# Moving preparation steps between the down-projection stages of a fused ConvFFN kernel

## The chip, the cores and the metric

The kernel runs on one core of one Trainium2 chip. Its time is the device time of one execution in microseconds (us), given as the median of several runs. A profiled execution, taken by the hardware profiler, supplies the trace: its span runs from the first to the last instruction.

## The reference, cut to what matters

One decoder layer over 512 prompt tokens and 8 x 8 sample tokens (576 columns in all, width 1024). What the change touches is the last part, a convolutional feed-forward network (2816 hidden columns, 22 tiles of 128), and, by way of the scheduler, the attention.

```python
def _layer(x, c, ...):
    h = _rmsnorm(x, norm1_g) * (1.0 + sc1) + sh1
    b_gate, c_gate, xa, q, k, v, ga, gb = jnp.split(h @ w_in, cuts, axis=-1)
    ...                                          # short convolution, attention, two gates
    x = x + g1 * (mixed @ w_mix_out)
    h2 = _rmsnorm(x, norm2_g) * (1.0 + sc2) + sh2
    a, val = jnp.split(h2 @ w_up, 2, axis=-1)
    ac, new_ffn = _causal_conv(a, ffn_buf, ffn_conv_w)       # 3 taps per channel
    x = x + g2 * ((jax.nn.gelu(ac, approximate=False) * val) @ w_down)
    return x, ...
```

All is float32.

## The kernel before, in words

**Layout.** Activations lie transposed: 128 channels on the partitions, the 576 tokens along the free axis. A float32 product is made of three TensorE passes in `fp32r`: each operand is split into a high part (`hi`, a copy rounded to fp32r) and a low part (`lo`, what the rounding left), and hi x hi, hi x lo and lo x hi are added up in PSUM.

**Seven products for eight.** The feed-forward works on pairs: two weight tiles by the two halves of the tokens (288 columns each), and two halves of the summed axis. `pair_product` does such a block with seven products where the plain way takes eight, from sums and differences of weights (A, B, C, D) and of activations. It runs seven *parts*, numbered 0 to 6, in three PSUM banks: X, Z, Y, X, Y, Z, Y. Y is a row `mm` in the profile, X and Z are `aux`; a copy of Z in SBUF is `p` (`p5`). Between the parts, small operations carry one bank into another:

| after part | operation | row in the profile | what needs it |
|---|---|---|---|
| 0 | ACT, `minus(Y, X)`: Y becomes -X | `mm<-aux` | part 2, which adds into Y |
| 1 | ACT, copy of Z to `p5` | `p<-aux` | `minus(Z, Y)`, which writes Z; the outputs after parts 4 and 5 |
| 2 | ACT, `minus(Z, Y)`: Z becomes -Y | `aux<-mm` | part 4, which adds into Y; part 5, which adds into Z |
| 3 | DVE, `out_a0(X)` | `x<-aux` in down stages | |
| 4 | DVE, `out_b1(Y, p5)` reads Y | `p<-mm` in down stages | part 6, which adds into Y |
| 5, 6 | DVE, `out_a1(Z, p5)`, `out_b0(Y)` | | |

In up stages a part is 12 matmuls, in down stages 9.

**Steps.** A stage's `steps[k]` are emitted ahead of part k (`steps[7]` after the last). Here stands the work for the *next* stage: its weights are read, summed and split while this stage multiplies. `pair_weights(ra, rb, moved)` gives the pieces: `ah`/`al` the high and low part of A (from `ra`), `sums1` two DVE sums (D's, and B's, in place in `rb`), `bh`/`bl` B, `sums2` two more DVE sums for C, `dh`/`dl` D (half as wide; rows `wh`, `wl`, `s`), `ch`/`cl` C. A high part is one ACT copy (`whi<-raw`). A low part is a DVE subtraction (`wlo<-raw,whi`). For a name in `moved` it is made without DVE: ACT writes minus the high part (`wlo<-whi`), then a DMA that POOL issues adds the raw weights to it (the profile's DMA row `wlo<-raw`, or `wl<-s` for D); I call it that name's *transfer*.

**The stages.** `order` runs the up tiles 4 to 10 (each with a gate and a value half), then four down stages m = 0, 2, 4, 6 over the first six hidden tiles (`FA = 6`), then the up tiles 11 to 21. An up stage's work beside the product comes from `beside_pair`: A at step 0, B's high part at 1, its low part at 2, D from 3, C at 5, and between them the convolution of the tile before: `first_tap` (ACT, `y<-pad,par2T`), `taps` (two DVE operations, `y<-pad,par2T,y`), `gelu`, `times`, `high`. A down stage's work comes from `beside_down(t, summed)`: the first down stage makes `sums1` itself (`summed` false); the other three find it made, at step 6 of the stage before. Tile 10's convolution is left over when the down stages begin; `first_ops` puts its taps into the second down stage and its GELU and multiplication into the third.

**What sets the order.** From the feed-forward on, PE, ACT and DVE are *pinned*: they run their instructions in the order in which the code emits them, by the helper at line 115 (so nearly every profile row has line 115). An instruction that waits thus holds all behind it on its engine. The parts before, the attention among them, are ordered by a scheduler's estimates, which know the pools of buffers. Tiles of 576 columns come from one pool of `A_BUFS` buffers (*slots*), taken in turn; a taker waits until the last user of its slot is done. Four raw weight tiles (`raw`) and five each of `whi` and `wlo` are in flight.

Of the kernel before, what the change touches and what calls it, by code (L numbers as in the profile page):

```python
# [10 lines left out]
F32 = mybir.dt.float32  # L11
# [5 lines left out]
P = 128  # L17
D = 1024
# [11 lines left out]
DOWN_AT = 11  # L30
# [6 lines left out]
CACHE_AT = 17,18  # L37
EPS = 1e-6
NEG = -1e33
A_BUFS = 57  # L40
W_BUFS = 4
S_BUFS = 5
HT = NT // 2
# [32 lines left out]
def step_kernel(ctx: ExitStack, tc: tile.TileContext, ins: dict, outs: list):  # L76
# [4 lines left out]
    cp = ctx.enter_context(tc.tile_pool(name="cp", bufs=1))  # L81
    ap_ = ctx.enter_context(tc.tile_pool(name="ap", bufs=A_BUFS))
    wp = ctx.enter_context(tc.tile_pool(name="wp", bufs=3))
# [12 lines left out]
    def slot(s, dt=F32, shape=None):  # L96
        return ap_.tile(shape or [P, NT], dt, tag="a", name=nm(s))

    def mmps():
        return pm.tile([P, 1024], F32, tag="mm", name=nm("mm"))  # L100

    def aux():
        return pa.tile([P, 512], F32, tag="aux", name=nm("aux"))
# [18 lines left out]
    matmul, transpose = pe.matmul, pe.transpose  # L122
# [34 lines left out]
    def split_w(raw):  # L157
        nk = raw.shape[1]
        hi = wp.tile([P, nk, P], F32R, tag="whi", name=nm("whi"), bufs=S_BUFS)
        lo = wp.tile([P, nk, P], F32R, tag="wlo", name=nm("wlo"), bufs=S_BUFS)  # L160
        split(hi, lo, raw)
        return (lambda k: hi[:, k, :]), (lambda k: lo[:, k, :])
# [386 lines left out]
    par = cp.tile([88, P], F32, tag="par", name="par")  # L549
# [53 lines left out]
    last_load = ada1_load(3)  # L603
    ident = cp.tile([P, P], F32, tag="ident", name="ident")
    make_identity(nc, ident)
    ones = cp.tile([P, P], F32, tag="ones", name="ones")
    nc.gpsimd.memset(ones, 1.0)
    mhalf = cp.tile([P, 8], F32, tag="mhalf", name="mhalf")
    nc.gpsimd.memset(mhalf, -0.5)
# [11 lines left out]
    def rows_rsqrt(out, src, n=P):  # L621

        dve.tensor_scalar(
            out=out, in0=src, scalar1=1.0 / D, scalar2=EPS, op0=ALU.mult, op1=ALU.add
        )
        pool.tensor_tensor(out=out, in0=out, in1=mhalf[:n, : out.shape[1]], op=ALU.pow)
# [226 lines left out]
    for j in (2, 0, 1):  # L853
        t = slot("kT")
# [33 lines left out]
    def tok_cols(t, i):  # L888

        at = i * P if i < 4 else NT - P  # L890
        return t[:, at : at + P]
# [17 lines left out]
    for i in (3, 4):  # L909
        a = aux()  # L910
        for j in range(2):
            transpose(a[:, j * P : j * P + P], tok_cols(kT[j], i), ident)
        t = slot("kout", shape=[P, 256])
# [77 lines left out]
    nc.vector.reduce_sum(out=snks, in_=sel, axis=AX.X)  # L991
    nsnks = cp.tile([P, 4], F32, tag="nsnks", name="nsnks")
    nc.vector.tensor_scalar(out=nsnks, in0=snks, scalar1=-1.0, scalar2=None, op0=ALU.mult)
    par2 = cp.tile([74, P], F32, tag="par2", name="par2")
    for dst, src in (
        (par2[:66], ins["ffn_conv_w"].rearrange("o a (r c) -> (o a r) c", c=P)),
        (par2[66:], ins["final_g"].rearrange("(r c) -> r c", c=P)),
# [477 lines left out]
    for at, m in enumerate(PLAIN):  # L1475
        if at in (4, 5):
            src, dst = ((ins["cache_k_win"], nks), (ins["cache_v_win"], nvs))[at - 4]
# [23 lines left out]
        if at == 1:  # L1501
            a = aux()
# [92 lines left out]
    for n, m in enumerate(turn):  # L1595
# [16 lines left out]
        t = gb.pop(m)  # L1612
# [35 lines left out]
    acc = slot("acc")  # L1648
# [70 lines left out]
    def norm2_rows(g):  # L1719
        a = aux()  # L1720
        i0, i1 = (0, 2) if g == 0 else (2, 5)
        for i in range(i0, i1):
            matmul(a[:, 2 * i : 2 * i + 2], tok_cols(acc, i), ones[:, 0:2], start=True, stop=True)
        src = a[:, 2 * i0 : 2 * i1].rearrange("p (i e) -> p i e", e=2)[:, :, 0]
        rows_rsqrt(r2[:, i0:i1], src)

# [44 lines left out]
    up_weights(1)  # L1771
    pinned.append(pe)
    mix_late(NK - 3, 1, (NORM2[0], lambda: norm2_rows(0)))
    R = {}
    ahead = []
# [179 lines left out]
    def merged(*parts):  # L1955

        out = {}
        for at in range(8):
            fs = [f for p in parts for f in p.get(at, [])]
            if fs:  # L1960
                out[at] = lambda fs=fs: [f() for f in fs]
        return out

    def beside_pair(p, t):

        none = lambda: None
        f = lambda n: t[n] if t else none
        g = lambda n: getattr(p, n) if p else none
        return {
            0: [f("ah"), g("first_tap"), f("sums1"), f("al"), g("taps")],  # L1970
            1: [f("bh")],
            2: [f("bl")],
            3: [g("gelu"), f("dh"), f("sums2")],
            4: [f("dl")],
            5: [f("ch"), g("times"), f("cl")],
            6: [g("high")],
            7: [g("low")],
        }

    def beside_down(t, summed):  # L1980

        f = lambda n: t[n]
        return {
            0: [f("ah")] + ([] if summed else [f("sums1")]) + [f("al")],
            2: [f("bh")],
            3: [f("bl"), f("sums2")],
            4: [f("dh"), f("dl")],
            5: [f("ch"), f("cl")],
        }

    def down_load(m, m0, m1):
        return load_w(kpm(w_dn, m * P, m0, m1 - m0), m1 - m0)
# [110 lines left out]
    def raw_op(kp, *names):  # L2103
        def f():
            if kp not in ops_d:
                ops_d[kp] = RawOperands(fr[2 * kp], fr[2 * kp + 1], made_d)
            for name in names:
                getattr(ops_d[kp], name)()
        return f
# [12 lines left out]
    def turned(w):  # L2122
        return tuple((lambda k, part=part: part((k + AWAY) % (FB - FA))) for part in w)
# [5 lines left out]
    stages = {0: pair, 1: nxt}  # L2129
    up_last = {}  # L2130
# [7 lines left out]
        ("up", 10): {1: [raw_op(2, "first_low")], 4: [raw_op(2, "second")], 6: [raw_op(1, "third")],  # L2138
                     7: [raw_op(2, "second_low"), raw_op(1, "third_low")]},
        ("down", 0): {0: [raw_op(2, "third", "third_low")]},  # L2140
        ("down", 2): {0: [lambda: up_last["p"].first_tap(), lambda: up_last["p"].taps()]},
        ("down", 4): {3: [lambda: up_last["p"].gelu()], 5: [lambda: up_last["p"].times()],
                      6: [lambda: up_last["p"].high()]},
    }
    before, prepared = None, {}
    for n, at in enumerate(order):
        job = stages.pop(n)
        beside = []
        if n == 0:
            beside.append({  # L2150
                1: n3, 2: [tiles[3].gelu], 5: [lambda: tiles[3].times(v3)],
                6: [tiles[3].high, tiles[3].low],
            })
        ahead, own = first_ops.get(at, {}), {}
        if n + 2 < len(order):
            kind, m = order[n + 2]
            stages[n + 2] = FfnPair(m) if kind == "up" else DownPair(m)
        if n + 1 < len(order):
            if at[0] == "up":
                own = beside_pair(before, stages[n + 1].prepare("BD" if n + 1 < DOWN_AT else ""))  # L2160
                beside += [own, ahead]
            else:
                summed = n + 1 in prepared
                t = prepared.pop(n + 1) if summed else stages[n + 1].prepare("BD")
                beside += [ahead, beside_down(t, summed)]
                if order[n + 1][0] == "down":
                    prepared[n + 2] = stages[n + 2].prepare("BD")
                    beside.append({6: [prepared[n + 2]["sums1"]]})
        else:
            raw = [down_load(j, FA, FB) for j in range(4)]  # L2170
            beside.append(beside_pair(before, None))
            beside.append({2: [lambda: wd.update({0: turned(split_w(raw[0]))})], 3: [fetch],
                           5: [lambda: wd.update({1: turned(split_w(raw[1]))})], 6: [split_back]})
# [7 lines left out]
    def summed(m, c0=0, c1=NT, last=False):  # L2181

        sq = acc3 if m == 0 else slot("sq")
        act.activation(sq[:, c0:c1], x1[m][:, c0:c1], AF.Square)
        if m and not last:
            dve.tensor_tensor(
                out=acc3[:, c0:c1], in0=acc3[:, c0:c1], in1=sq[:, c0:c1], op=ALU.add
            )
        x = x1[m][:, c0:c1]
        act.activation(x, x, AF.Copy, scale=par2T[:, 66 + m : 67 + m])  # L2190
        return sq

    def final_rows(g, sq=None):

        a = mmps()
        i0, i1, step = (0, 2, 512) if g == 0 else (2, 5, 2)
        parts = [acc3] if sq is None else [acc3, sq]
        for n, x in enumerate(parts):
            for i in range(i0, i1):
                dst = a[:, (i - i0) * step : (i - i0) * step + 2]  # L2200
                matmul(dst, tok_cols(x, i), ones[:, 0:2], start=n == 0, stop=n == len(parts) - 1)
        src = a[:, : (i1 - i0) * step].rearrange("p (i e) -> p i e", e=step)[:, :, 0]
        rows_rsqrt(r3[:, i0:i1], src)

# [59 lines left out]
    for n, job in enumerate(jobs):  # L2264
# [11 lines left out]
        sums2 = {x: [lambda m=m: summed(m)] for x, m in after.items()}  # L2276
# [19 lines left out]
    def others():  # L2296
        final_rows(1)
        for i in (2, 3):
            tt = TokenTile(i)
            tt.turn(range(NK))  # L2300
            tt.finish((nc.sync, nc.sync))
# [44 lines left out]
```

## Time and profile before

| | |
|---|---|
| median of 3 runs | 959.73 us (959.21 to 961.36) |
| the profiled execution, its own time | 961.17 us |
| its span | 959.4 us, granted TensorE clock 0.999 |
| instructions | 18914 |
| busy share of the span | PE 98%, PE weight load 94%, DVE 76%, ACT 60%, POOL 16% |
| DMA | 155.70 MB, mean 162 GB/s |

How to read the rows that follow. A row of the *timeline* has the start in us from the span's start, the length (from the first start to the last end where it groups several, `x2`), the engine, the line, the operation with output<-inputs and their shapes, and in brackets how long the engine had been idle before and what released it. A row of the *windows* view has a stretch of time and its length, then the busy time of PE, PE's weight loads, DVE, ACT and POOL with the number of instructions in brackets, then the granted clock, the DMA engines' busy share and the GB/s they moved. A row that has a queue's name, such as `POOLq`, is from the list of DMAs: how often, how large, and the median from issue to landing.

The stages around the change lie at 610.55 (tile 4), 677.62 (tile 10), 688.74, 697.75, 708.25 and 716.59 (the four down stages) and 725.23 us (tile 11).

### The profile page before, as it was taken

The numbers are of one execution on the slowest core, as the hardware profiler recorded it, in microseconds if no ns is written. First come the engines' busy times: TensorE is split into PE (matmuls) and PEld (weight loads), VectorE is DVE, ScalarE is ACT, GpSimd is POOL, SyncE is SP. The second block draws the span as 40 slices with busy tenths as digits, with TensorE's granted clock in tenths as the row PEclk, the third lists the DMA queues.
The fourth block names the chain that finished last, engine by engine and source line by source line (L and its number), as shares of the span: only waits on it lengthen the run. The fifth ranks groups of instructions, "written<-read, shape, count | busy, mean of one in ns | idle before, by whom it ended". The sixth has DMA issues, their size and how long they took to land.

```text
span 959.4 us, 18914 instructions
## 1 busy us (share of the span) xinstructions
PE 939.6 (98%) x7254; PEld 903.3 (94%) x7254; DVE 732.8 (76%) x1391; ACT 576.3 (60%) x1106; POOL 154.7 (16%) x344
## 2 busy tenths in 40 slices
PE   6999999999999999999999999999999999999997
PEld 5799999999999899999889999999999999999996
DVE  5688988875866867876677588788888989876663
ACT  5375767745665447865344576677755655585364
POOL 2222121101201012210001130122321011111110
PEclk9999999999999999999999999999999999999999
DMA  9984333426546768899985732377676333377432
GB/s 284 323 250 108 82 87 100 140 80 173 122 128 201 236 221 208 204 240 288 306 283 113 186 86 78 83 175 186 150 161 168 89 108 91 98 196 171 103 87 99
DMA packets 187068, 155.70 MB, mean 162 GB/s; under 512 B 8328, under 2 KB 163276, under 8 KB 186690
## 3 DMA queue, kind: packets, MB, share of 16 engines
q1 hardware_dynamic: 173394, 113.19, 39.7%
q0 software_dynamic: 13440, 41.04, 19.5%
q8 instruction: 57, 0.93, 0.4%
q14 instruction: 33, 0.27, 0.1%
q10 hardware_dynamic: 144, 0.26, 0.1%
HBM read 115.36 MB, written 13.55 MB: 134 GB/s over the span
## 4 chain that ended last, share of the span: by engine, by line
PE 89%; DMA 3%; ACT 3%; DVE 2%; issue 1%; SPq 1%; ACTq 0%; DVEq 0%
PE mm L115 50%; PE aux L115 37%; PE aux L1284 2%; PE aux L1188 2%; DMA ad<-in_w_ada 1%; SPq L541 1%; ACT whi L115 1%; DMA wlo<-raw 1%; DMA q<-low 1%; ACT wlo L115 1%; DMA wl<-s 0%; ACT xh L115 0%; DMA cs<-in_c_prompt 0%; ACT aux L115 0%; ACT sg L115 0%
## 5 line engine op out<-in xcount | busy, mean ns | idle before, releaser
L115 ACT ACTIVATE whi<-raw 128x1024 fp32r<-128x1024 f32 (+3 forms) x190 | 191.9, 1018 | 50.3 <-DVE raw L115 20.0
L115 DVE TENSOR_TENSOR wlo<-raw,whi 128x1024 fp32r<-128x1024 f32 (+3 forms) x156 | 182.3, 1174 | 37.3 <-ACT whi L115 36.9
L115 PE MATMUL aux<-2h,whi 128*128 128x288 f32 (+2 forms) x232 | 68.5, 295 | 0.0
L115 PE MATMUL aux<-2l,whi 128*128 128x288 f32 (+2 forms) x232 | 68.4, 295 | 0.0
L115 PE MATMUL aux<-2h,wlo 128*128 128x288 f32 (+2 forms) x232 | 68.4, 295 | 0.0
L115 DVE TENSOR_TENSOR raw<-raw 128x512 f32<-128x512 f32 (+1 forms) x96 | 65.9, 686 | 3.1
L115 POOL DMA_DIRECT2D wlo<-raw x34 | 29.4, 866 | 210.0 <-ACT wlo L115 88.7
L115 PE MATMUL mm<-hh,whi 128*128 128x256 f32 (+2 forms) x264 | 60.6, 303 | 0.5 <-ACT hh L115 0.5
L115 PE MATMUL mm<-hh,wlo 128*128 128x256 f32 (+2 forms) x264 | 58.3, 295 | 0.0
L115 PE MATMUL aux<-hh,whi 128*128 128x288 f32 (+1 forms) x196 | 57.5, 300 | 0.0
L115 PE MATMUL mm<-hl,whi 128*128 128x256 f32 (+2 forms) x264 | 57.4, 296 | 0.1
L115 PE MATMUL aux<-hl,whi 128*128 128x288 f32 (+1 forms) x196 | 56.5, 295 | 0.0
L115 PE MATMUL aux<-hh,wlo 128*128 128x288 f32 (+1 forms) x196 | 56.5, 295 | 0.0
L115 PEld LDWEIGHTS mm<-hh,whi 128*128 128x128 f32 x264 | 43.8, 189 | 1.4 <-ACT hh L115 1.0
L115 PEld LDWEIGHTS mm<-hh,wlo 128*128 128x128 f32 x264 | 44.6, 188 | 0.0
L115 PEld LDWEIGHTS mm<-hl,whi 128*128 128x128 f32 x264 | 44.0, 188 | 0.7 <-DVE hl L115 0.5
L115 PEld LDWEIGHTS aux<-2h,whi 128*128 128x128 f32 x232 | 43.7, 189 | 0.0
L115 PEld LDWEIGHTS aux<-2h,wlo 128*128 128x128 f32 x232 | 43.7, 188 | 0.0
L115 PEld LDWEIGHTS aux<-2l,whi 128*128 128x128 f32 x232 | 43.7, 188 | 0.0
L115 ACT ACTIVATE aux<-mm 128x288 f32<-128x288 f32 x48 | 19.0, 395 | 37.7 <-PE mm L115 36.9
L115 ACT ACTIVATE mm<-aux 128x288 f32<-128x288 f32 x45 | 17.9, 397 | 39.3 <-PE aux L115 39.3
L115 DVE SCALAR_TENSOR_TENSOR y<-pad,par2T,y 128x592 f32<-128x592 f32 x44 | 36.6, 833 | 6.2 <-ACT y L115 5.5
(412 smaller groups left out, 3261.3 us busy)
## 6 DMA issues: line engine op xcount, KB each, us to landing
raw<-in_w_in SPq DMA_DIRECT2D x52, 512.0 KB, 4.7
raw<-in_w_up SPq DMA_DIRECT2D x44, 512.0 KB, 4.1
ada<-in_w_ada SPq DMA_DIRECT2D x64, 256.0 KB, 5.6
wlo<-raw POOLq DMA_DIRECT2D x30, 512.0 KB, 5.1
ad<-in_w_ada SPq DMA_DIRECT2D x32, 256.0 KB, 6.3
raw<-in_w_down SPq DMA_DIRECT2D x16, 512.0 KB, 4.8
wl<-s POOLq DMA_DIRECT2D x23, 256.0 KB, 4.1
sg_dram<-sg POOLq DMA_DIRECT2D x16, 288.0 KB, 4.3
```

The costliest lines, as they stand in the source:

```text
L115: done = getattr(self.engine, name)(*args, **kwargs)
L541: return tc.keep_in_program_order(nc.sync.dma_start(dst, src))
L1188: done = nc.tensor.matmul(O[HALF[par], c], vt(i - nkt + 1 + kt)[:, hd * 64 : hd * 64 + 64], pts[kt][:, par * 256 : par * 256 + 256], start ...
L1284: done = nc.tensor.matmul(ps[32 * j : 32 * j + 32, :], cT[:, k, :], cols[k][j], start=(k == 1), stop=(k == NK - 2),)
```

## The change

Six edits:

- `beside_down` has a new table. In the stages whose first sums are ready (the second to the fourth down stage), B's high part goes from step 2 to step 1, its low part from step 3 to step 2. In the first down stage, A goes from step 0 to step 1.
- Tile 10's `first_tap` and `taps` go from step 0 to step 4 of the second down stage.
- Beside the first up pair (tile 4, where tile 5's weights are prepared) only D is made by transfer; B's low part there is a DVE subtraction.
- The pool of slots has 58 buffers instead of 57.
- `ones` has 2 columns instead of 128; only two were ever read.
- `par2` shares the buffer of `par`.

```diff
-A_BUFS = 57
+A_BUFS = 58
...
-    ones = cp.tile([P, P], F32, tag="ones", name="ones")
+    ones = cp.tile([P, 2], F32, tag="ones", name="ones")
...
-    par2 = cp.tile([74, P], F32, tag="par2", name="par2")
+    par2 = cp.tile([88, P], F32, tag="par", name="par2")[:74]
...
     def beside_down(t, summed):
 
-        f = lambda n: t[n]
-        return {
-            0: [f("ah")] + ([] if summed else [f("sums1")]) + [f("al")],
-            2: [f("bh")],
-            3: [f("bl"), f("sums2")],
-            4: [f("dh"), f("dl")],
-            5: [f("ch"), f("cl")],
-        }
+        at = [["ah", "al"], ["bh"], ["bl"], ["sums2"], ["dh", "dl"], ["ch", "cl"]]
+        if not summed:
+            at = [[], ["ah", "sums1", "al"], ["bh"], ["bl", "sums2"], ["dh", "dl"], ["ch", "cl"]]
+        return {n: [t[x] for x in names] for n, names in enumerate(at)}
...
-        ("down", 2): {0: [lambda: up_last["p"].first_tap(), lambda: up_last["p"].taps()]},
+        ("down", 2): {4: [lambda: up_last["p"].first_tap(), lambda: up_last["p"].taps()]},
...
-                own = beside_pair(before, stages[n + 1].prepare("BD" if n + 1 < DOWN_AT else ""))
+                moved = "" if n + 1 >= DOWN_AT else "BD" if n else "D"
+                own = beside_pair(before, stages[n + 1].prepare(moved))
```

ACT in the second down stage, before. `whi<-raw` is A's copy at step 0, the second `whi` and `wlo<-whi` are B's, `mm<-aux`, `p<-aux` and `aux<-mm` are the product's own:

```order
L115 ACTIVATE y_8929<-pad_8651,par2T 128x592
L115 ACTIVATE whi_8933<-raw_8796 128x768
L115 ACTIVATE mm_8926<-aux_8925 128x288
L115 COPY p_8928<-aux_8927 128x288
L115 ACTIVATE whi_8957<-raw_8799 128x768
L115 ACTIVATE aux_8927<-mm_8926 128x288
L115 ACTIVATE wlo_8958<-whi_8957 128x768
```

And now:

```order
L115 ACTIVATE whi_8928<-raw_8795 128x768
L115 ACTIVATE mm_8925<-aux_8924 128x288
L115 ACTIVATE whi_8942<-raw_8798 128x768
L115 COPY p_8927<-aux_8926 128x288
L115 ACTIVATE wlo_8943<-whi_8942 128x768
L115 ACTIVATE aux_8926<-mm_8925 128x288
L115 ACTIVATE y_8979<-pad_8650,par2T 128x592
```

The first tap has gone from the head of the stage to behind `aux<-mm`; B's copy stands ahead of `p<-aux` and its low copy ahead of `aux<-mm`. The third and the fourth stage differ in the same way in B's two copies.

DVE in the second down stage, before, from B's sum on (it is made at the end of the stage before); `x<-mm` is an output of the first stage, `wlo` A's low part, the two `raw` are `sums2`, `x<-aux` the output after part 3, `p<-mm` the read of Y after part 4:

```order
L115 TENSOR_TENSOR raw_8799<-raw_8799 128x384
L115 SCALAR_TENSOR_TENSOR x_6532<-mm_8803,modT,x_6532 128x288
L115 SCALAR_TENSOR_TENSOR y_8929<-pad_8651,par2T,y_8929 128x592 x2
L115 TENSOR_TENSOR wlo_8934<-raw_8796,whi_8933 128x768
L115 TENSOR_TENSOR raw_8796<-raw_8796,raw_8799 128x384
L115 TENSOR_TENSOR raw_8796<-raw_8796 128x384
L115 SCALAR_TENSOR_TENSOR x_6532<-aux_8925,modT,x_6532 128x288
L115 TENSOR_TENSOR p_8998<-mm_8926,p_8928 128x288
```

And now:

```order
L115 TENSOR_TENSOR raw_8798<-raw_8798 128x384
L115 SCALAR_TENSOR_TENSOR x_6532<-mm_8802,modT,x_6532 128x288
L115 TENSOR_TENSOR wlo_8929<-raw_8795,whi_8928 128x768
L115 TENSOR_TENSOR raw_8795<-raw_8795,raw_8798 128x384
L115 TENSOR_TENSOR raw_8795<-raw_8795 128x384
L115 SCALAR_TENSOR_TENSOR x_6532<-aux_8924,modT,x_6532 128x288
L115 SCALAR_TENSOR_TENSOR y_8979<-pad_8650,par2T,y_8979 128x592 x2
L115 TENSOR_TENSOR p_8997<-mm_8925,p_8927 128x288
```

The two taps have moved from ahead of A's low part to right ahead of `p<-mm`.

In the attention, DVE's order is the scheduler's. Before, around the two pairs of `low` (low parts of q, each pair followed by a DMA `q<-low`; `wlo` is a weight's low part, `nmx` a softmax maximum):

```order
L946 SCALAR_TENSOR_TENSOR low_2316<-qt_2137,q_2317 64x512
L946 SCALAR_TENSOR_TENSOR low_2316<-qt_2137,q_2318 64x512
L1022 TENSOR_REDUCE nmx_2275<-s_2259 128x2
L1022 TENSOR_REDUCE nmx_2275<-s_2260 128x2
L115 TENSOR_TENSOR wlo_2850<-raw_2847,whi_2849 128x1024
L946 SCALAR_TENSOR_TENSOR low_2327<-qt_2138,q_2328 64x512
L946 SCALAR_TENSOR_TENSOR low_2327<-qt_2138,q_2329 64x512
```

And now:

```order
L1022 TENSOR_REDUCE nmx_2275<-s_2259 128x2
L1022 TENSOR_REDUCE nmx_2275<-s_2260 128x2
L115 TENSOR_TENSOR wlo_2850<-raw_2847,whi_2849 128x1024
L946 SCALAR_TENSOR_TENSOR low_2316<-qt_2137,q_2317 64x512
L946 SCALAR_TENSOR_TENSOR low_2316<-qt_2137,q_2318 64x512
L1025 TENSOR_TENSOR nmx_2275<-nmx_2275,nsnk 128x4
L946 SCALAR_TENSOR_TENSOR low_2327<-qt_2138,q_2328 64x512
L946 SCALAR_TENSOR_TENSOR low_2327<-qt_2138,q_2329 64x512
```

Both pairs of `low` now stand behind the weight's subtraction, the second close behind the first.

More of the change, by code (lines that the diff above doesn't have):

```diff
@@ L1722, in norm2_rows @@
         for i in range(i0, i1):
-            matmul(a[:, 2 * i : 2 * i + 2], tok_cols(acc, i), ones[:, 0:2], start=True, stop=True)
+            matmul(a[:, 2 * i : 2 * i + 2], tok_cols(acc, i), ones, start=True, stop=True)
         src = a[:, 2 * i0 : 2 * i1].rearrange("p (i e) -> p i e", e=2)[:, :, 0]
@@ L2200, in final_rows @@
                 dst = a[:, (i - i0) * step : (i - i0) * step + 2]
-                matmul(dst, tok_cols(x, i), ones[:, 0:2], start=n == 0, stop=n == len(parts) - 1)
+                matmul(dst, tok_cols(x, i), ones, start=n == 0, stop=n == len(parts) - 1)
         src = a[:, : (i1 - i0) * step].rearrange("p (i e) -> p i e", e=step)[:, :, 0]
```

## The prediction

> **What bounds the kernel now.** I read the page first (span, engines, chain), then the stages around the change one by one in the windows view, then the timeline of each engine where a stage is too long.
>
> ```profile
> span 959.4 us, 18914 instructions
> PE 939.6 (98%) x7254; PEld 903.3 (94%) x7254; DVE 732.8 (76%) x1391; ACT 576.3 (60%) x1106; POOL 154.7 (16%) x344
> PE 89%; DMA 3%; ACT 3%; DVE 2%; issue 1%; SPq 1%; ACTq 0%; DVEq 0%
> ```
>
> TensorE (PE) is busy for 98% and carries 89% of the chain that ended last. The number of its multiplications does not change, so the time can only move by what PE waits. The windows view shows where it does near the change, one row a stage: tile 4, tile 10, the four down stages in order, tile 11. The second number is the stage's length.
>
> ```profile
> 610.55:622.09 11.54, 11.37 (x87) 11.13 (x85) 7.13 (x15) 6.94 (x13) 2.34 (x6) 1.00 0.44 96
> 677.62:688.74 11.12, 11.12 (x87) 11.12 (x86) 9.41 (x19) 8.18 (x15) 3.17 (x7) 1.00 0.75 176
> 688.74:697.75 9.01, 8.87 (x66) 8.40 (x65) 7.92 (x16) 6.34 (x12) 1.72 (x2) 1.00 0.46 118
> 697.75:708.25 10.50, 8.58 (x65) 8.35 (x64) 8.91 (x19) 6.45 (x11) 1.71 (x2) 1.00 0.63 141
> 708.25:716.59 8.34, 8.34 (x66) 8.34 (x64) 7.31 (x19) 5.90 (x10) 2.05 (x3) 1.00 0.80 185
> 716.59:725.23 8.64, 8.64 (x66) 8.41 (x64) 8.40 (x17) 5.76 (x9) 3.08 (x8) 1.00 0.97 224
> 725.23:737.96 12.73, 11.37 (x87) 11.14 (x86) 10.91 (x19) 4.39 (x7) 2.17 (x3) 1.00 0.73 172
> ```
>
> Tile 10's 11.12 us is an undisturbed up stage, the third down stage's 8.34 us an undisturbed down stage; a part is a seventh of it, 1.59 and 1.19 us. Over these, tile 4 loses 0.42, the down stages 0.67, 2.16, 0 and 0.30, and tile 11 loses 1.61: 5.16 us in all. That is the most the edits to these stages can win. The granted clock is 1.00 throughout, so a wait costs its own length and a restart of about 0.1 (below).
>
> **The change part by part.** *First pair, D alone by transfer.* B's low part in tile 4's stage goes from ACT and POOL to DVE.
>
> ```profile
> 615.81 1.05 ACT L115 ACTIVATE wlo<-whi 128x1024 fp32r<-128x1024 f32 x1
> 616.75 0.41 ACT L115 ACTIVATE aux<-mm 128x288 f32<-128x288 f32 x1
> 617.21 0.41 PE L115 MATMUL mm<-2h,wh 128*128 128x288 f32 x1 [0.17 <-ACT aux L115]
> 619.19 0.52 DVE L115 TENSOR_TENSOR pad<-mm,p 128x224 f32<-128x224 f32 x2 [3.18 <-PE mm L115]
> ```
>
> PE starts part 4 when ACT has copied the negated Y to Z (`aux<-mm`), and ACT is 1.05 us late because of the copy before it. Without that copy PE does not wait: -0.42. The subtraction that DVE takes instead is 1.22 us (the row `wlo<-raw,whi` in the last fence of this part) and fits into DVE's 3.18 us of idling. POOL loses one transfer; SP's and POOL's queues have nothing else moved there. Bounds -0.42 and +0.1 (if DVE delays the adds that C waits for).
>
> *First down stage, A's copy a step later.*
>
> ```profile
> 690.15 0.84 ACT L115 ACTIVATE whi<-raw 128x768 fp32r<-128x768 f32 x1
> 690.88 0.40 ACT L115 ACTIVATE mm<-aux 128x288 f32<-128x288 f32 x1
> 691.34 0.40 PE L115 MATMUL mm<-th,whi 128*128 128x288 f32 x1
> 691.58 0.29 PE L115 MATMUL mm<-tl,whi 128*128 128x288 f32 x1
> ...
> 692.88 0.85 ACT L115 ACTIVATE whi<-raw 128x768 fp32r<-128x768 f32 x1 [1.16 <-DVE raw L115]
> 694.08 0.40 PE L115 MATMUL mm<-xh,wh 128*128 128x288 f32 x1
> ```
>
> Part 2 is due at 688.74 + 2 x 1.19 = 691.12 and starts at 691.34, right after ACT's `mm<-aux`, which stood behind A's copy. (After a wait the second matmul follows by 0.24 instead of 0.13: the restart's 0.1.) With the copy behind `mm<-aux`, part 2 starts when due. Part 4 waits for `aux<-mm` behind B's copy, which waits for DVE's adds; those move up with the rest. I take the whole 0.67; bounds 0 and -0.67. A's low part now follows a step later on DVE, with three parts in hand before it is used.
>
> *Second down stage, taps at step 4.*
>
> ```profile
> 699.58 0.56 DVE L115 TENSOR_TENSOR raw<-raw 128x384 f32<-128x384 f32 x1
> ...
> 700.33 0.79 ACT L115 ACTIVATE y<-pad,par2T 128x592 f32<-128x592 f32 x1 [3.57 <-DMA wl<-s]
> 701.02 0.83 ACT L115 ACTIVATE whi<-raw 128x768 fp32r<-128x768 f32 x1
> 701.75 0.39 ACT L115 ACTIVATE mm<-aux 128x288 f32<-128x288 f32 x1
> 702.20 0.40 PE L115 MATMUL mm<-th,whi 128*128 128x288 f32 x1 [1.92 <-ACT mm L115]
> ...
> 701.14 1.71 DVE L115 SCALAR_TENSOR_TENSOR y<-pad,par2T,y 128x592 f32<-128x592 f32 x2 [0.57 <-ACT y L115]
> 706.15 0.46 DVE L115 TENSOR_TENSOR p<-mm,p 128x288 f32<-128x288 f32 x1 [0.74 <-PE mm L115]
> ```
>
> The first tap's buffer becomes free only when D's transfer has landed; ACT idles 3.57 us for it, and A's copy and `mm<-aux` queue behind it. Step 4 comes four parts, 4.76 us, later, and the transfer has long landed then. So the 2.16 go. But the two taps on DVE, 1.71 us, now stand right ahead of `p<-mm`, the read of Y after part 4, and part 6 may not add to Y before that read. DVE's sum for B is ready at 700.14, 2.4 into the stage; ACT's `aux<-mm` then ends at 4.6 (2.2 later, worked out under the third stage below), the first tap at 5.3, the two taps at 7.0 and the read at 7.4, with overlaps of 0.1. Part 6 is due at 6 x 1.19 = 7.15: a wait of 0.3 to 0.4, with restart 0.5. Bounds 0 (the idle 0.74 swallows it) and 0.9. Next late is what follows on DVE: the read starts at 6.95 where it started 6.2 into the stage (706.15, less the start and the 2.16), and PE's own wait gives back 0.45, so 0.3 is left for the third stage.
>
> *B a step sooner, in stages 2 to 4.* B's copy and its negated low copy now both stand ahead of `aux<-mm`, which part 4 needs. Fourth stage:
>
> ```profile
> 714.46 0.46 DVE L115 TENSOR_TENSOR p<-mm,p 128x288 f32<-128x288 f32 x1 [0.74 <-PE mm L115]
> ...
> 719.38 0.69 DVE L115 TENSOR_TENSOR raw<-raw 128x512 f32<-128x512 f32 x1
> ...
> 719.33 0.40 ACT L115 COPY p<-aux 128x288 f32<-128x288 f32 x1 [0.96 <-PE aux L115]
> 720.11 1.07 ACT L115 ACTIVATE whi<-raw 128x1024 fp32r<-128x1024 f32 x1 [0.38 <-DVE raw L115]
> 721.07 0.40 ACT L115 ACTIVATE aux<-mm 128x288 f32<-128x288 f32 x1
> 721.40 1.04 ACT L115 ACTIVATE wlo<-whi 128x1024 fp32r<-128x1024 f32 x1
> ```
>
> DVE works without a gap from the read of Y in the stage before (714.46) to the sum that B's copy needs (ends 720.07, 3.48 into the stage). So B's copy cannot start before 3.52, wherever it stands in ACT's queue. Then come, each about 0.1 less than its duration because neighbours overlap: B's copy 0.97, `p<-aux` 0.30, the low copy 0.94, `aux<-mm` 0.40 in full. End 6.13; part 4 is due at 4 x 1.19 = 4.76. PE waits 1.4, with restart 1.5, where it lost 0.30 in all. Bounds 0.3 (if DVE's chain came 1.2 us earlier) and 1.9. In the third stage the weights are 768 wide (0.83 a copy, as at 701.02): B's copy starts at 2.4 + 0.05 + the 0.3 by which DVE is late, and 0.73 + 0.30 + 0.73 + 0.40 = 2.2 after it `aux<-mm` ends, at 4.9: a wait of 0.2, with restart 0.3 (0 to 0.7). In the second it ends at 4.6, before 4.76: no wait.
>
> Tile 11's wait:
>
> ```profile
> 722.74 5.82 DMA wlo<-raw
> ...
> 728.60 0.41 PE L115 MATMUL aux<-th,wlo 128*128 128x288 f32 x1 [1.36 <-DMA wlo<-raw]
> ...
> wlo<-raw POOLq DMA_DIRECT2D x30, 512.0 KB, 5.1
> ```
>
> The low copy ended at 722.44 and POOL issued 0.3 later. After the change the copy ends 5.8 into the fourth stage, the transfer is issued at 6.1 and lands at 11.9 if it takes 5.82 again, 11.2 at the median of 5.1. PE needs it 0.26 into part 1 of tile 11, at 8.34 + 1.5 + 1.59 + 0.26 = 11.7: a wait of 0.2, between 0 and 0.6, for 1.61 before. By the Trainium skill ("DMA: Bandwidth & Descriptors", Anatomy of one DMA, the GpSimd path) a transfer takes about 2.0 us and its bytes at 436 GB/s, which I estimate at 3.2 us for these 512 KB; then tile 11 would wait for nothing and the sum be 0.2 lower. The row of 5.82, and the wait it made, disagree with that, and the measurement decides.
>
> *58 slots, two columns of ones, `par2` in `par`'s place.* Same operations, smaller constants at the start, where the chain runs on loads; I cost them at nothing. But a slot more lets the scheduler reorder DVE and ACT in the attention, which is not pinned:
>
> ```profile
> 174.83 1.22 DVE L115 TENSOR_TENSOR wlo<-raw,whi 128x1024 fp32r<-128x1024 f32 x1
> 175.96 1.40 DVE L946 SCALAR_TENSOR_TENSOR low<-qt,q 64x512 fp32r<-64x512 f32 x2
> ...
> 176.93 5.04 DMA q<-low
> ...
> 182.11 0.30 PE L115 MATMUL aux<-kh,q 128*128 128x128 f32 x1 [0.48 <-DMA q<-low]
> ```
>
> PE waits for a transfer of q that starts late because `low` stands behind a 1.22 us weight subtraction. In the new order the first pair of `low` stands behind that subtraction and the second follows at once, with fewer reductions between; q would start up to 0.9 sooner. That is worth up to the 0.5 to 0.65 here, and other softmax steps move by a few tenths both ways. I take -0.6, between -1.1 (0.65 and 0.45 more elsewhere) and +0.7 (if another step that PE waits for comes behind a subtraction of 1.22 us, and half of that is covered).
>
> **Sum.** Gone: 5.16. New: 0.5 + 0.3 + 1.5 + 0.2 = 2.5. Attention -0.6. Together -3.26 us. The profiled span goes from 959.4 to 956.1; that execution took 961.17, its own time, 1.4 above the median of 959.73, and would be at 957.9. On the median: 956.5.
>
> **Rivals.** (1) *All waits go*: ACT is not late after all, because DVE's chain shrinks. Then 959.73 - 5.16 - 0.6 = 954.0. Against it: the chain from 714.46 to 720.07 is not touched by the edits. (2) *The attention gives nothing or costs*: 959.73 - 2.66 + 0 to 0.7 = 957.1 to 957.8. For it: the scheduler orders by estimates, and most attention waits are short. (3) *Traded one for one*: the tap still waits for its buffer at step 4, or the taps cost 1.71 instead of 0.5 and tile 11 still waits for B. With 1.2 and 1.4 more than above, and nothing from the attention, 959.7. Against it: the tap got its buffer at 700.33, and step 4 comes 4.76 into the stage, after 702.5 in the same clock. (4) *Slower*: the low copy ahead of `aux<-mm`, in all three stages. Each microsecond that B's copy starts later costs PE one in every stage from 2 to 4. Without the attention's gain the time is 957.1; it passes 961.65 when the three together lose 4.6 more, so when B's copy comes about 1.55 us later in each. The taps' 1.71 on DVE are a source for that in one stage only, and half of it is absorbed in PE's own wait.
>
> **How the numbers follow.** My forecast 0.56 (955.2 to 957.4 by its own bounds), rival 1 0.09, rival 2 0.18, rival 3 0.13, rival 4 0.04. A measurement of this kernel can tell about 0.2%, 1.9 us. Faster by more, below 957.8: forecast, rival 1 and most of rival 2, 0.78. Within: 0.17; slower: 0.05. The range reaches from 955.0, which leaves out most of rival 1, to 959.0, which leaves out rival 4 and half of rival 3.
>
> **What would show it.** Right: stages of 8.34 (first), about 8.8 (second, with a wait ahead of part 6), 8.6 and 9.9 (fourth, with PE waiting for ACT `aux` ahead of part 4), 11.1 for tile 4, 11.1 to 11.5 for tile 11; ACT's `y<-pad` without a wait for a transfer. Wrong: a fourth stage near 8.3; a tap that still waits; a PE wait for `q<-low` of 0.5 us or more, or a new one between 160 and 260 us.

## The result, and the profile after

| | before | after |
|---|---|---|
| median of 15 runs each | 960.52 us (958.96 to 962.70) | 958.05 us (957.26 to 959.38) |
| ratio, 95% interval | | 0.9974 (0.9967 to 0.9982) |
| span of the profiled execution | 959.4 | 956.0 |
| its own time | 961.17 | 958.05 |

The change makes the kernel 0.26% faster, 2.5 us, where 3.26 were forecast; 958.05 lies within the range of 955.0 to 959.0. Ratios here and below leave out slow executions, of which there were two in all: 1108.03 us with the taps alone and 3281.4 us with the first pair alone.

The head of the page after. TensorE is still the bound, with the same 7254 matmuls:

```profile
span 956.0 us, 18891 instructions
PE 940.4 (98%) x7254; PEld 904.8 (95%) x7254; DVE 734.3 (77%) x1392; ACT 575.1 (60%) x1105; POOL 152.3 (16%) x343
```

The windows of the same seven stages after: tile 4, tile 10, the four down stages, tile 11.

```profile
610.16:621.29 11.13, 11.13 (x86) 11.13 (x85) 8.36 (x16) 6.11 (x12) 1.54 (x5) 1.00 0.43 110
676.89:688.01 11.12, 11.12 (x86) 11.12 (x85) 9.40 (x19) 8.18 (x15) 3.47 (x7) 1.00 0.72 175
688.01:697.02 9.01, 8.59 (x65) 8.36 (x64) 7.90 (x16) 7.20 (x13) 1.75 (x2) 1.00 0.46 119
697.02:705.86 8.84, 8.63 (x65) 8.40 (x64) 8.48 (x19) 5.69 (x10) 1.72 (x2) 1.00 0.85 183
705.86:714.51 8.65, 8.62 (x66) 8.38 (x64) 7.49 (x19) 5.92 (x10) 2.04 (x3) 1.00 0.80 181
714.51:724.22 9.71, 8.62 (x66) 8.38 (x65) 8.65 (x17) 6.18 (x9) 2.76 (x7) 1.00 0.84 209
724.22:735.36 11.14, 11.14 (x87) 11.14 (x86) 10.47 (x19) 3.73 (x6) 1.40 (x2) 1.00 0.69 173
```

Against before, tile 4 gave 0.41 us, the first down stage nothing (9.01 in both), the second 1.66; the third lost 0.31 and the fourth 1.07; tile 11 gave 1.59. The waits of PE between 600 and 740 us, before and then after:

```profile
PE mm L115 <- ACT mm L115: 1.9, 1, 1.9
PE aux L115 <- DMA wlo<-raw: 1.4, 1, 1.4
PE mm L115 <- ACT aux L115: 0.2, 1, 0.2
```

```profile
PE mm L115 <- ACT aux L115: 1.5, 2, 1.1
PE mm L115 <- DVE p L115: 0.2, 1, 0.2
```

The waits for the first tap (`ACT mm`) and for tile 11's transfer are gone; in their place stand two waits for `aux<-mm` and one for `p<-mm`. The 1.1 in the fourth stage and the 0.2 in the second are where the prediction put them; the other 0.4 is in the first stage, where it had none. In the third stage part 4 starts 0.2 late, too little for this list. The last matmul starts 2.53 us earlier (949.71 for 952.24). The other 0.9 us of the spans' difference lies behind it, in the output, which the change does not touch: 7.2 us there in the profile of before, 6.1 to 6.4 in the thirteen others of this document.

The ACT copies of the fourth stage after, to be set against the ones of before:

```profile
717.88 1.06 ACT L115 ACTIVATE whi<-raw 128x1024 fp32r<-128x1024 f32 x1 [1.57 <-DVE raw L115]
718.85 0.38 ACT L115 COPY p<-aux 128x288 f32<-128x288 f32 x1
719.12 1.06 ACT L115 ACTIVATE wlo<-whi 128x1024 fp32r<-128x1024 f32 x1
720.08 0.40 ACT L115 ACTIVATE aux<-mm 128x288 f32<-128x288 f32 x1
```

B's copy starts 3.37 into the stage (3.52 forecast) and `aux<-mm` ends at 5.97 (6.13 forecast), where part 4 was due at 4.76.

### The profile page after: what moved, and what is told of

It is laid out like the page before. It is cut to its first block, busy times and chain, and to the rows that moved or that the text cites. A ratio compares the mean times of both kernels' runs of the same rounds, so it can differ in the third digit from the quotient of the medians.

```text
span 956.0 us, 18891 instructions
## 1 busy us (share of the span) xinstructions
PE 940.4 (98%) x7254; PEld 904.8 (95%) x7254; DVE 734.3 (77%) x1392; ACT 575.1 (60%) x1105; POOL 152.3 (16%) x343
```

## The experiments

### One edit at a time

**The taps alone.**

```diff
-        ("down", 2): {0: [lambda: up_last["p"].first_tap(), lambda: up_last["p"].taps()]},
+        ("down", 2): {4: [lambda: up_last["p"].first_tap(), lambda: up_last["p"].taps()]},
```

> The kernel before with one edit alone: tile 10's first tap and taps at step 4 of the second down stage. Theory (the first tap held ACT until a slot came free, and A's copy and mm<-aux stood behind it): the second stage goes from 10.50 to 8.7 to 8.9 us, with a wait of 0.3 to 0.5 ahead of part 6 where DVE's two taps stand ahead of p<-mm; the first (9.01), third (8.34), fourth (8.64) and tile 11 (12.73) stay. In all -1.7 us. Rival (the stage is long because of B's copies, not the tap): 10.5 stays, 0 us.

Measured: 958.20 us, ratio 0.9973 (0.9959 to 0.9987). The second stage is 9.32 us: the wait for the first tap is gone, but the one ahead of part 6 is 0.7 and not 0.3 to 0.5. ACT's first tap comes behind B's low copy here, and DVE waits for it:

```profile
704.05 1.71 DVE L115 SCALAR_TENSOR_TENSOR y<-pad,par2T,y 128x592 f32<-128x592 f32 x2 [0.20 <-ACT y L115]
705.89 0.46 DVE L115 TENSOR_TENSOR p<-mm,p 128x288 f32<-128x288 f32 x1
```

In the whole change B's low copy stands further ahead and the taps cost 0.5, not 1.0. With the same order but 57 slots (below) they cost 0.7, so that B's place accounts for some 0.3 of this and the slots for the rest.

**The table alone.**

```diff
     def beside_down(t, summed):
...
+        at = [["ah", "al"], ["bh"], ["bl"], ["sums2"], ["dh", "dl"], ["ch", "cl"]]
+        if not summed:
+            at = [[], ["ah", "sums1", "al"], ["bh"], ["bl", "sums2"], ["dh", "dl"], ["ch", "cl"]]
+        return {n: [t[x] for x in names] for n, names in enumerate(at)}
```

> The kernel before with the new table of beside_down alone. Theory (a low copy ahead of aux<-mm costs a wait in the stage, and frees tile 11's): tile 11 from 12.73 to 11.1 (-1.6), the fourth stage from 8.64 to 9.7 (+1.05), the third 8.3 to 8.6, the second still 10.4 to 10.5 (the tap holds ACT as before), the first still 9.0 (its wait only moves from part 2 to part 4, because B's sum on DVE is no earlier). In all -0.3 to -0.6 us. Rival (the first stage was bound by ACT's order): first stage 8.34, -1.2 us in all.

Measured: 961.73 us, ratio 1.0007 (0.9994 to 1.0021): no gain. The stages are 8.54, 10.53, 8.38 and 9.85, tile 11 is 11.09; the profiled execution, 959.01, is one of its two fastest. The first stage was expected at 9.0: what differs from before there is taken up below. As expected, tile 11's wait is traded against the fourth stage's, and the tap waits as ever (ACT's row in the second stage, with a slot that D's transfer holds):

```profile
699.42 0.79 ACT L115 ACTIVATE y<-pad,par2T 128x592 f32<-128x592 f32 x1 [3.60 <-DMA wl<-s]
```

**The first pair alone.**

```diff
-                own = beside_pair(before, stages[n + 1].prepare("BD" if n + 1 < DOWN_AT else ""))
+                moved = "" if n + 1 >= DOWN_AT else "BD" if n else "D"
+                own = beside_pair(before, stages[n + 1].prepare(moved))
```

> The kernel before with one edit alone: beside tile 4 only D is made by transfer. Theory: tile 4's stage from 11.54 to 11.12, nothing else moves, -0.4 us. Rival (DVE's subtraction delays C's sums and with them the next stage): tile 4 or tile 5's stage at 11.4 or more, 0 us.

Measured: 959.31 us, ratio 0.9982 (0.9971 to 0.9994). Tile 4's stage is 11.09, so its 0.4 is there. The profile also shows the first stage at 8.66 and tile 11 at 11.45, where this kernel does nothing else than before. So two of the stage lengths in the one profile of before, 9.01 and 12.73, are not what this code always gives. By its interval the kernel is 0.6 to 2.8 us faster than before, more than the 0.4 that the edit was to bring; where the rest comes from is not shown.

**The slots alone.**

```diff
-A_BUFS = 57
+A_BUFS = 58
...
-    ones = cp.tile([P, P], F32, tag="ones", name="ones")
+    ones = cp.tile([P, 2], F32, tag="ones", name="ones")
...
-    par2 = cp.tile([74, P], F32, tag="par2", name="par2")
+    par2 = cp.tile([88, P], F32, tag="par", name="par2")[:74]
```

> The kernel before with 58 slots, ones as two columns and par2 in par's buffer, and nothing else. Theory: the attention's order changes as in the changed kernel, PE's wait of 0.48 for q<-low goes, and tile 4 starts 0.3 to 0.6 us earlier; the first down stage stays at 9.0. The second stage tells whether a slot more would have been enough: 10.5 if the first tap still takes a slot that a transfer holds, about 9 if the ring hands it another one. In all -0.4 us in the first case, -1.9 in the second. Rival (the attention's gain is no gain): tile 4 starts within 0.15 of 610.55.

Measured: 957.82 us, ratio 0.9969 (0.9958 to 0.9980): as much as the whole change (0.9974), which goes for the taps alone (0.9973) as well. The second stage, with the taps still at step 0, is 8.66 instead of 10.50 (windows view, first to fourth down stage):

```profile
689.10:697.75 8.65, 8.59 (x66) 8.36 (x65) 7.90 (x16) 7.26 (x14) 1.71 (x2) 1.00 0.49 128
697.75:706.41 8.66, 8.61 (x66) 8.37 (x65) 8.38 (x19) 5.81 (x10) 1.72 (x2) 1.00 0.78 173
706.41:714.75 8.34, 8.34 (x66) 8.34 (x65) 7.49 (x19) 5.96 (x10) 2.31 (x3) 1.00 0.76 178
714.75:723.36 8.61, 8.61 (x66) 8.43 (x64) 8.37 (x18) 5.89 (x9) 3.02 (x7) 1.00 1.00 228
```

One slot more shifts the ring by one, and the first tap gets a slot that no transfer holds: it starts at 696.82, while D's transfer lands at 700.17. The prediction had costed this edit at nothing in these stages.

### The change with one edit taken back

**Taps at step 0 again.**

```diff
-        ("down", 2): {4: [lambda: up_last["p"].first_tap(), lambda: up_last["p"].taps()]},
+        ("down", 2): {0: [lambda: up_last["p"].first_tap(), lambda: up_last["p"].taps()]},
```

> The changed kernel with tile 10's taps back at step 0 of the second down stage. Theory (with 58 slots the first tap no longer takes a slot that a transfer holds): no long wait ahead of part 2; the second stage 8.6 to 8.9, and the others as in the changed kernel, 0 +- 0.3 us. Rival (the move of the taps is what took away the 2 us): the second stage back at 10 or more, +1.5 us.

Measured: 957.54 us, ratio 0.9959 (0.9947 to 0.9971). The second stage is 8.65, the fourth 9.71; the first is 8.33. The first tap does not wait for D's transfer, which lands at 698.50:

```profile
695.09 0.79 ACT L115 ACTIVATE y<-pad,par2T 128x592 f32<-128x592 f32 x1 [0.36 <-DVE rt L115]
```

So with 58 slots the move of the taps gains nothing more; either of the two edits takes the 2 us wait away.

**57 slots again** (`A_BUFS = 57`, all else as changed).

> The changed kernel with 57 slots instead of 58. Theory (the stretch from 150 to 610 us is the slots' part of the change): from 150.9 us of before to tile 4 takes 459.0 to 459.8 instead of 458.9, with the mix around 405 us 0.5 longer; tile 4 11.13, second stage 8.8 to 8.9 because the tap comes later, third, fourth and tile 11 as in the changed kernel; first stage 8.4 to 9.0 by the away transfer's landing. In all +0.3 to +0.9 us against the changed kernel. Rival (the mix's 0.5 has another cause): no difference from 150 to 610 us.

Measured: 957.50 us, ratio 0.9959 (0.9947 to 0.9971): not slower, where 0.3 to 0.9 us slower than the change was expected. The first two stages are 9.19 and 9.04, a little over what was expected. The mix around 405 us is 0.5 longer, as expected, but the stretches beside it are shorter by as much: from before's 150.9 us to tile 4 this profile takes 458.95 us, for 458.92 after. Over all profiles with 57 slots that stretch takes 459.64, 459.82, 459.01, 459.06 and 458.95; in the nine with 58 it is 458.90 to 458.93. The two long ones are those in which PE waits for q; its waits in the attention before, and with the taps alone:

```profile
PE aux L115 <- DMA q<-low: 0.5, 1, 0.5
```

```profile
PE aux L115 <- DMA q<-low: 0.7, 1, 0.7
```

The matmul that waited before (182.11 in the prediction) is this one after, with no wait:

```profile
182.71 0.27 PE L115 MATMUL aux<-kh,q 128*128 128x128 f32 x1
```

Counted from the stretch's start, the transfer that it needs starts at 26.0 us with 57 slots and at 25.6 with 58, and PE comes to the matmul at 30.6 and at 31.5. With 57 slots PE waited where this transfer took 5.04 and 5.26 us, not where it took 3.82, 3.85 and 4.49; with 58 it took up to 5.12 without a wait. So the new order of the attention hardly makes the stretch shorter by itself; it takes out a wait that comes when the transfer is long.

**B's low copy late, in the fourth stage alone** (`late` is true there).

```diff
+        if late:
+            at = [["ah", "al"], ["bh"], [], ["bl", "sums2"], ["dh", "dl"], ["ch", "cl"]]
```

> The changed kernel with B's low copy back at step 3 in the fourth down stage alone, behind aux<-mm. Theory (a trade: the copy's 1.0 us stands either ahead of part 4 or ahead of tile 11's transfer): the fourth stage from 9.71 to 8.6 to 8.8, and tile 11 from 11.14 to 11.5, since the transfer, issued 6.1 to 6.3 into the stage, takes 4.6; in all -0.6 to -0.8 us. Rival (tile 11's wait is what the profile of before showed): tile 11 at 12.7, +0.6 us.

Measured: 958.34 us, ratio 0.9965 (0.9952 to 0.9977). The fourth stage is 8.88, tile 11 is 11.65: 0.3 better than the change's 9.71 and 11.14 together, where 0.6 to 0.8 were expected. The median does not tell it from the change. The profile's first stage, which this kernel leaves as changed, is 10.33. The row behind that is in the next part.

### The first stage

After, DVE in the first stage: `nl` is the last of tile 10's operands, `s` and `raw` are the two sums.

```profile
689.90 0.45 DVE L115 TENSOR_TENSOR nl<-cy,nh 128x288 fp32r<-128x288 f32 x1
690.98 0.56 DVE L115 TENSOR_TENSOR s<-raw,raw 128x384 f32<-128x384 f32 x1 [0.63 <-DMA away<-cy]
691.57 0.56 DVE L115 TENSOR_TENSOR raw<-raw 128x384 f32<-128x384 f32 x1
```

DVE waits, with nothing in the data calling for it, for the transfer that puts tile 9's product away: the sum `s` is to be written into that product's slot. B's copy and `aux<-mm` follow on ACT, and part 4 waits. In the profile with B's low copy late the same row is:

```profile
692.19 0.56 DVE L115 TENSOR_TENSOR s<-raw,raw 128x384 f32<-128x384 f32 x1 [1.95 <-DMA away<-cy]
```

Before, DVE already idled at this place, one subtraction earlier, at `nl`. The first row is of before; the second is the same instruction in the changed kernel with 57 slots:

```profile
691.33 0.46 DVE L115 TENSOR_TENSOR nl<-cy,nh 128x288 fp32r<-128x288 f32 x1 [0.61 <-ACT mm L115]
690.17 0.46 DVE L115 TENSOR_TENSOR nl<-cy,nh 128x288 fp32r<-128x288 f32 x1 [0.79 <-DMA away<-cy]
```

The first names ACT, but `nl` does not read `mm`, and in both `away<-cy` landed 0.10 ahead of the start (691.23 and 690.07). So the wait of before was very likely the transfer's as well. With the old table and an early landing the stage is 8.66 (taps alone, first pair alone), with the new one 8.54 (table alone).

Five kernels have this stage as changed, with 58 slots. The landing is that of `away<-cy`, from the stage's start:

| kernel | transfer, us | landed | stage |
|---|---|---|---|
| sums ahead of C (below) | 3.2 | 2.00 | 8.33 |
| taps at step 0 | 3.2 | 2.05 | 8.33 |
| the change | 4.1 | 2.95 | 9.01 |
| taps behind the read (below) | 4.2 | 3.03 | 9.09 |
| low copy late | 5.4 | 4.27 | 10.33 |

From about 2.3 on, a later landing lengthens the stage by as much; before that it costs nothing. **The two sums earlier**, at step 6 of tile 10's stage:

```diff
+            if at == ("up", DOWN_AT - 1):
+                prepared[n + 2] = stages[n + 2].prepare("BD")
+                beside.append({6: [prepared[n + 2]["sums1"]]})
...
-            at = [[], ["ah", "sums1", "al"], ["bh"], ["bl", "sums2"], ["dh", "dl"], ["ch", "cl"]]
+            at = [[], ["ah", "al"], ["bh"], ["bl", "sums2"], ["dh", "dl"], ["ch", "cl"]]
```

> The changed kernel, and in addition the first down stage's two sums (D's and B's for the second stage) at step 6 of tile 10's stage instead of step 1 of its own. Theory (in the first stage B's sum is late because DVE waits for a slot that the away transfer holds until 690.95, so B's copy and aux<-mm behind it are late): B's copy starts about 1 us earlier, part 4 waits for nothing, the first stage goes from 9.01 to 8.34 and the time falls by 0.7 us. Rival (ACT's own row of copies is what is late): 9.0 stays.

Measured: 958.23 us, ratio 0.9975 (0.9964 to 0.9987); the first stage is 9.02. The theory's 8.34 is missed, and the rival's 9.0 comes about in another way than it says: PE no longer waits at part 4, but the slot has gone to an operand that ACT writes ahead of `mm<-aux`, so part 2 waits, 0.6 us with a transfer of 3.2:

```profile
690.01 0.45 ACT L115 ACTIVATE nh<-cy 128x288 fp32r<-128x288 f32 x1 [0.97 <-DMA away<-cy]
690.36 0.39 ACT L115 ACTIVATE mm<-aux 128x288 f32<-128x288 f32 x1
```

The wait belongs to the slot, not to the instruction: whoever is next in the ring takes it over.

### Why the third and fourth stages wait

**The sums ahead of C**, at step 5 instead of 6:

```diff
-                beside += [ahead, beside_down(t, summed)]
+                early = []
+                beside += [{5: early}, ahead, beside_down(t, summed)]
...
-                    beside.append({6: [prepared[n + 2]["sums1"]]})
+                    early.append(prepared[n + 2]["sums1"])
```

> The changed kernel, and in addition the next stage's two sums at step 5 ahead of tile 10's times and C's two parts, instead of step 6, in the first three down stages. Theory (ACT's low copy ahead of aux<-mm costs a wait only because B's sum comes late from DVE): the sums move up by 1.3 us or more, the fourth stage goes from 9.71 to 8.34 to 8.6 and the third from 8.65 to 8.34; the second keeps its wait of 0.5. C's low part is later by about 1.3 and is the next thing to be late, at part 2: up to 0.3 in one stage. In all -1.2 to -1.7 us. Rival (the copies on ACT alone fill the time up to part 4): the fourth stage stays above 9.4.

Measured: 956.36 us, ratio 0.9950 (0.9937 to 0.9963), the lowest median of all. Windows of the first to the fourth stage and of tile 11:

```profile
688.24:696.57 8.33, 8.33 (x65) 8.33 (x64) 7.78 (x17) 7.21 (x13) 1.75 (x2) 1.00 0.50 129
696.57:705.38 8.81, 8.60 (x65) 8.37 (x64) 8.50 (x18) 5.78 (x10) 1.71 (x2) 1.00 0.85 182
705.38:713.72 8.34, 8.34 (x65) 8.34 (x64) 7.48 (x17) 6.02 (x10) 2.02 (x3) 1.00 0.89 200
713.72:722.37 8.65, 8.62 (x65) 8.39 (x64) 8.42 (x18) 6.09 (x9) 2.73 (x7) 1.00 0.95 231
722.37:733.50 11.13, 11.13 (x86) 11.13 (x85) 10.76 (x19) 3.74 (x6) 1.40 (x2) 1.00 0.63 166
```

ACT has the same copies in the same order, and the fourth stage loses 0.3 instead of 1.4, the third nothing. (The first stage's 8.33 for 9.01 is another 0.7 us, which came of an early landing, as above.) In the fourth stage B's copy now starts 1.72 after the stage's start, and `aux<-mm` ends at 4.32, before part 4 is due:

```profile
715.44 1.05 ACT L115 ACTIVATE whi<-raw 128x1024 fp32r<-128x1024 f32 x1
...
717.63 0.41 ACT L115 ACTIVATE aux<-mm 128x288 f32<-128x288 f32 x1
```

So the low copy ahead of `aux<-mm` costs only where B's sum is late from DVE, which is how the prediction put it.

**The taps behind the read of Y.**

```diff
-        ("down", 2): {4: [lambda: up_last["p"].first_tap(), lambda: up_last["p"].taps()]},
+        ("down", 2): {4: [lambda: up_last["p"].first_tap()], 5: [lambda: up_last["p"].taps()]},
```

> The changed kernel, with the two taps on DVE at step 5 of the second stage, behind the read of Y, and the first tap on ACT still at step 4. Theory (DVE is full here, and what is taken from one wait is given to the next): the second stage's wait ahead of part 6 goes (8.84 to 8.4), and the third stage's sums come about 1.1 us later against its start, so its wait ahead of part 4 grows from 0.3 to 1.2 to 1.5; in all +0.5 to +0.9 us. Rival (DVE has slack enough): the third stage stays at 8.65, -0.4 us.

Measured: 959.16 us, ratio 0.9981 (0.9971 to 0.9991). The second stage falls to 8.39, the third goes from 8.65 to 9.96, the fourth from 9.71 to 9.92. The sums for the third stage now follow the 1.7 us of taps on DVE: what is taken from one wait is given to the next, with 1.1 on top.

**All three** (the first sums early, the others ahead of C, the taps behind the read and the sums).

> The changed kernel with the three edits together: the first stage's sums at tile 10's step 6, the others at step 5 ahead of C, the taps at step 5 behind the sums' place of the stage (ahead of C). Theory: first stage 8.34, second and third 8.34 to 8.6 each, fourth 8.8 to 9.1, where DVE is now without a gap and its read of Y ahead of part 6 is 0.5 late; -1.7 to -2.2 us against the changed kernel. Rival (one of the waits is only handed on): less than -1 us, with 1 us or more in one stage.

Measured: 957.91 us, ratio 0.9976 (0.9961 to 0.9990): no better than the change's 0.9974. The profiled execution, 956.88, is the fastest of ten that reach up to 961.56; its last matmul is 1.1 us earlier than after the change. Stages of 8.92, 8.36, 8.63 and 8.93: the second to fourth about as expected, the first with the slot's wait again, and so less in all than the 1.7 to 2.2 us.

**The best of it**: the sums ahead of C, the taps at step 0, and in the first stage the sums ahead of tile 10's third operands, so that the slot falls to `nl`, which only part 6 needs. The diff is against the kernel with the sums ahead of C; the line of the taps is as above.

```diff
-            at = [[], ["ah", "sums1", "al"], ["bh"], ["bl", "sums2"], ["dh", "dl"], ["ch", "cl"]]
+            at = [[], ["ah", "al"], ["bh"], ["bl", "sums2"], ["dh", "dl"], ["ch", "cl"]]
...
-                beside += [{5: early}, ahead, beside_down(t, summed)]
+                beside += [{0: [] if summed else [t["sums1"]], 5: early}, ahead, beside_down(t, summed)]
```

> The kernel of the run with the sums ahead of C, with two more edits: the taps back at step 0 of the second down stage (58 slots hand the first tap a slot that no transfer holds), and in the first stage the two sums ahead of tile 10's third operands, so that the slot of the away transfer falls to the last subtraction (nl), which part 6 needs, and not to B's chain. Theory: first stage 8.34 whatever the away transfer takes, second 8.6 to 8.7 (as with 58 slots alone), third 8.34, fourth 8.65, tile 11 11.13; 0.1 to 0.8 us faster than with the sums ahead of C alone, 4.3 to 5 faster than before. Rival (the wait follows the slot to another engine, as with the early first sums): first stage 8.7 or more.

Measured: 956.81 us, ratio 0.9950 (0.9937 to 0.9962). Here the transfer took 5.0 us and landed 3.80 into the stage, which by the table above would have made it 8.33 + 1.5 = 9.8 in the changed order; it is 8.56, with DVE's wait at `nl`:

```profile
692.31 0.46 DVE L115 TENSOR_TENSOR nl<-cy,nh 128x288 fp32r<-128x288 f32 x1 [0.94 <-DMA away<-cy]
```

The second stage was 8.94, more than the 8.65 expected, because DVE brought 1 us of delay along. This kernel was to be 0.1 to 0.8 us faster than the kernel with the sums ahead of C alone, but on the median the two can't be told apart; both are faster than the change, whose interval starts at 0.9967.

## Why the prediction was right, and where it was not

- *Tile 4*: -0.42 forecast, -0.41 measured, and 11.09 with that edit alone.
- *First down stage*: -0.67 forecast, 0 in the profile. The failed step is "Part 4 waits for `aux<-mm` behind B's copy, which waits for DVE's adds; those move up with the rest." They could not move up: DVE waits for the slot's transfer, which landed at 2.95 into the stage. The row of before in which DVE idles 0.61 at `nl` was passed over. Where it landed at 2.0, the stage was the 8.33 forecast. The part on part 2 held, since its wait is gone.
- *Second stage*: 8.8 forecast, 8.84 measured, with the wait ahead of part 6. The tap got its slot, but "I cost them at nothing" was wrong of the 58 slots: they alone make 8.66, and with them the move of the taps adds nothing.
- *Third and fourth stage*: 8.6 and 9.9 forecast, 8.65 and 9.71 measured, and the sums ahead of C show that DVE's chain is the cause. Rival 1, *all waits go*, is out by these rows, rival 4 by B's copy, which starts no later than forecast (3.37 for 3.52 in the fourth stage), and rival 3 by the first tap, which does not wait at step 4.
- *Tile 11*: a wait of 0.2 forecast, none measured: the transfer was issued 5.97 into the stage, 6.1 forecast, and took 4.7, less than either of the durations that the prediction took from rows (5.82 and 5.1). The gain, though, was sized on an exception. "1.61 before" comes from a transfer of 5.82; the three kernels that keep that part of the code and issue it as late (the taps, the first pair and the slots alone) have 4.5 to 4.6 and a stage of 11.45 to 11.51, so that the wait is worth some 0.35. By the Trainium skill ("DMA: Bandwidth & Descriptors", Anatomy of one DMA, the GpSimd path), about 2.0 us and the bytes at 436 GB/s, I estimate 3.2 us for it. None of the runs shows that: the fourteen profiles have 4.5 to 5.8.
- *Attention*: -0.6 forecast, and the profiles differ by 0.72 there. The mechanism holds in part: the transfer starts sooner, by 0.45 us where up to 0.9 was said. What the prediction missed is that the new order also brings PE to the matmul 0.9 later, so that the gain is no more than the wait for q, which only some executions of before have. With 57 slots and the rest changed the stretch is as short as with 58. So rival 2, *the attention gives nothing or costs*, is not out: it forecast a gain of 1.9 to 2.6 us, and the medians give 2.5.

The sum also adds up what does not add up. The taps alone and the slots alone each give as much as the whole change, and both take away the 2 us wait of the second stage; the table alone gives nothing.

With the exceptions taken out, what the profile pair shows is -0.41, 0, -1.66, +0.31, +1.07 and -0.35, together -1.0, and up to -0.7 in the attention. The medians differ by 2.5. The 0.7 or more that lie between are not settled: of before there is one profile, and its runs spread over 3.7 us (after: 2.1). Its waits for q, in the second stage and in tile 11 end with the landing of a transfer, and so, very likely, does the one in the first. The forecast gain was 0.8 us too large against these medians, and two terms are more than enough for it: the first stage's 0.67, and tile 11's 1.41 where 0.35 is the rule. These two come to 1.7, so about 0.9 of the measured gain is not in the sum as it was argued, and that the sum came so near is partly luck. (The forecast time was 1.5 too low; the other 0.8 is the median of before, 960.52 over 15 runs where it stood at 959.73 over 3.)

## What to carry to other kernels

When an instruction waits for a transfer that its data does not need, look at the buffer ring first: one buffer more or fewer, or another order of taking them, moves the wait to another instruction, and the best place for it is one that nothing waits for soon. A wait read from one profile is one draw of a DMA's duration; before taking it as a gain, see how long the same transfer takes elsewhere in the trace, and how the execution stands to the median. An engine that feeds another is worth reordering before the fed one: moving two sums up on DVE took 1.4 us out of the third and fourth stages, while moving B's copies up on ACT alone brought nothing. And edits that take away the same wait do not add up: measure each alone, and the whole with one of them taken back.

## What the runs showed of the hardware

The 288 KB transfer `away<-cy` at the first down stage took from 3.03 to 5.42 us in fourteen profiles of nearly the same program. In the five kernels that have this stage as changed, with 58 slots, it took 3.2 to 5.4, and the stage was 8.33 to 10.33 us by its landing. The 512 KB transfer ahead of tile 11 took 4.5 to 4.8 in thirteen of them and 5.8 once.
